# Strassen branch products: weight sums by accumulating DMAs in place of GpSimd, and the first operands split during attention

## The chip, the cores and the metric

One core of one Trainium2 chip. The metric is the device time of one execution in microseconds, as the median of several runs. TensorE (PE) multiplies matrices, VectorE (DVE), ScalarE (ACT) and GpSimd (POOL) work element by element, SyncE (SP) issues most of the loads and stores; 16 DMA engines carry them.

## The reference

One layer of a hybrid decoder: 1024 tokens, width 1024, float32. After a norm and a common input projection a state-space mixer gives `y_ssm` (width 2048) and latent attention gives `y_mla` (8 heads of 128). What the change touches is what joins them:

```
mixed = sigmoid(g_ssm) * (y_ssm @ w_branch_ssm) + sigmoid(g_mla) * (y_mla @ w_branch_mla)
h = h + mixed @ w_out
```

Norm, a two-layer MLP and a final norm follow. `w_branch_ssm` is 2048x1024 and `w_branch_mla` 1024x1024.

## The kernel before, in words

All matrix products run in float32 accuracy from pieces: every operand is split into a high part (a rounded copy, ACT, L69) and a low part (source less high part, VectorE, L70; together `split_sbuf`), and one float32 matmul is three matmuls, high by high, high by low, low by high (`mm`, L100). The stages follow one another: input projection, state-space mixer, gates, attention, branch products, out product, MLP.

**Attention** (L617 to L791) runs over 8 heads and in each over 4 pairs of 128-query tiles: scores (`sc`, `sx`), softmax on VectorE and ACT (`pr`), transposes of the probabilities on TensorE (`pp`, L737), their split (`pT`, by ACT L112 and VectorE L113), products with the values (`po`), a copy `oT` (ACT, L748), and a store to `d_o` in HBM, issued by GpSimd (L749). The state-space result lies in HBM as `d_y`, the gates as `d_g`.

**Branch products** (L798 to L943). Three products of 1024 rows of weights by 1024 tokens: `strassen(w, src, sink)` for the upper half of `w_branch_ssm` (`w_bs`) with the first half of y, the lower half with the second, and `w_branch_mla` (`w_bm`) with `d_o`. Each is cut into 2 x 2 blocks and done by seven products of 512 x 512 x 512 instead of eight, a Winograd form: F, E, G, E, G, E, E, where F, E, G are groups of four PSUM banks into which products accumulate (`pz`). A product is 48 matmuls of 128x512, 1008 in all. Its weights come as two units of 128x1024 (`st`, loaded by SP in `raw_unit` L822), its columns as two tiles `yr` (loaded in `columns` L854). Some products need sums of blocks: of the columns these are made on VectorE, of the weights on GpSimd, both in `combined` (L839): a22 + a21, then differences with a11, a12, a21, eight GpSimd instructions of 128x1024 in each `strassen`, 24 in all. `split_unit` and the `x` tiles then hold the parts; `whl` has four buffers, the units of two products; the raw weights lie in `wr` (7 buffers) and `stage` (3).

After a product, `done` hands its four banks to a sink. `set_mix` (L917) and `add_mix` (L923) write or add to `mix` in SBUF (ACT L919, VectorE L925). In the third `strassen` `gated_mix` (L931) multiplies by the gates, loaded as `g`: the sum so far once (VectorE, L935), the bank into `c` (VectorE, L937), and GpSimd adds `c` to `mix` (L938).

**Out product** (`out_row`, L985): `m`, the parts of 128 tokens of `mix` (ACT L989, VectorE L990), by `w_out`, into banks `pout`.

A scheduler of the framework sets the order of the instructions on each engine from the program's order, priorities and pools; an engine, SP's and GpSimd's queues too, takes its own instructions strictly in that order. A tile waits for the last reader of the buffer that it takes over: the pool `wr` lies where attention's tiles lay, so a first load into some of its buffers waits for the stores of `oT`.

Of the kernel before, what the change touches and what calls it, by code (L numbers as in the profile page):

```python
# [29 lines left out]
QH, NOPE, ROPE, DV = 8, 128, 64, 128  # L30
# [9 lines left out]
def hybrid_block(ctx: ExitStack, tc: tile.TileContext, a: dict):  # L40
    nc = tc.nc
    pe, act, dve, pool, sp = nc.tensor, nc.scalar, nc.vector, nc.gpsimd, nc.sync
# [7 lines left out]
    stage = ctx.enter_context(tc.tile_pool(name="stage", bufs=3))  # L50
    whl = ctx.enter_context(tc.tile_pool(name="whl", bufs=4))
# [119 lines left out]
    with ExitStack() as pa:  # L171
# [426 lines left out]
    xs = conv_x(0, first_pairs)  # L598
# [8 lines left out]
    for g in range(NG):  # L607
# [4 lines left out]
        if g + 1 < NG:  # L612
            xs = conv_x(g + 1) + conv_bc(g + 1)
    ssd.close()
    up.close()

    ring_stack = ctx.enter_context(ExitStack())  # L617
    ring_q = ring_stack.enter_context(tc.tile_pool(name="ring_q", bufs=4, reuse_waits="tile"))


    with ExitStack() as at:
# [153 lines left out]
        for n in range(4 * QH):  # L775
            h, b = divmod(n, 4)
            if b == 0 and h % 2 == 0:
                vt = values(shared["wv"], h % 4)
            scores_up_to(2 * n + 3)
            steps = weighted_values(h, b, prs[2 * n : 2 * n + 2], vt, h % 2)  # L780
            for _ in range(b + 2 >> 1):
                next(steps)
            scores_up_to(2 * n + 4)
            for _ in steps:
                pass
            if b == 1 and h + 1 < QH:
                heads_in[h + 1] = project(h + 1)
            if b == 1 and h + 2 == QH:
                at0.close()
                xr = ring_stack.enter_context(tc.tile_pool(name="xr", bufs=2, reuse_waits="tile"))  # L790
                yr = ring_stack.enter_context(tc.tile_pool(name="yr", bufs=8, reuse_waits="tile"))  # L791

# [1 line left out]


    ps2 = ctx.enter_context(ExitStack())  # L798
    pz = ps2.enter_context(tc.tile_pool(name="pz", bufs=8, space=PSUM, reuse_waits="tile"))
    with tc.using_default_side("right"):  # L800
        sm_stack = ctx.enter_context(ExitStack())
        sm = sm_stack.enter_context(tc.tile_pool(name="sm", bufs=1, reuse_waits="tile"))
# [1 line left out]
        wr = br.enter_context(tc.tile_pool(name="wr", bufs=7, reuse_waits="tile"))  # L804
# [3 lines left out]

    mix = [sm.tile([P, 8, 512], F32, name=f"mix{t}") for t in range(2)]

    def bank():
        return pz.tile([P, 512], F32, tag="z", name="pz")

    def split_unit(src):
        w = whl.tile([P, 2, 1024], F32R, tag="w", name="w")
        split_sbuf(w[:, 0, :], w[:, 1, :], src)
        return w

    def raw_unit(pl, src, k, tag):

        st = pl.tile([P, 1024], F32, tag=tag, name="st")
        sp.dma_start(out=st.rearrange("p (k c) -> p k c", k=k), in_=src.rearrange("(k p) c -> p k c", p=P))  # L822
        return st

    nx, nw = [0], [0]

    def raw_weights():
        nw[0] += 1
        return (wr, "wr") if nw[0] % 10 >= 3 else (stage, "st")

    def x_tile():
        nx[0] += 1
        if nx[0] % 6 in (1, 2):
            return xr.tile([P, 2048], F32R, tag="x", name="x")
        return ring_q.tile([P, 2112], F32R, tag="ring", name="x")[:, :2048]

    def combined(eng, op, outs, xs, ys):
        for o, x, y in zip(outs, xs, ys):
            eng.tensor_tensor(out=o, in0=x, in1=y, op=op)  # L839

    def strassen(w, src, sink):
        def weights(r, c):
            outs = []
            for q in range(2):
                pl, tag = raw_weights()
                outs.append(raw_unit(pl, w[512 * r : 512 * (r + 1), 512 * q + 256 * c : 512 * q + 256 * (c + 1)], 4, tag))
            return outs

        def columns(r, c):
            outs = []  # L850
            for kk in range(2):
                st = yr.tile([P, 1024], F32, tag="y", name="yr")
                k0 = 4 * r + 2 * kk
                sp.dma_start(  # L854
                    out=st.rearrange("p (k c) -> p k c", k=2), in_=src[:, k0 : k0 + 2, 512 * (1 - c) : 512 * (2 - c)]
                )
                outs.append(st)
            return outs

        def product(out, ws, xs, start):  # L860
            xv = []
            for x in xs:
                t = x_tile()
                split_sbuf(t[:, :1024], t[:, 1024:], x)
                xv.append(t.rearrange("p (j k c) -> p j k c", j=2, k=2))
            for g in range(2):
                wv = split_unit(ws[g]).rearrange("p j (k c) -> p j k c", k=4)
                for q in range(2):
                    o, cs = out[2 * g + q], slice(P * q, P * (q + 1))
                    for k in range(4):  # L870
                        wh, wl = wv[:, 0, k, cs], wv[:, 1, k, cs]
                        xh, xl = (xv[k // 2][:, j, k % 2, :] for j in (0, 1))
                        mm(o, wh, xh, start and k == 0, False, True)
                        mm(o, wh, xl, False, False, True)
                        mm(o, wl, xh, False, k == 3, True)

        def done(out, f, half, first):
            for g in range(2):
                for q in range(2):
                    sink(out[2 * g + q], 4 * g + 2 * f + q, 1 - half, first)  # L880

        sub, add = ALU.subtract, ALU.add
        a12, b21 = weights(1, 0), columns(1, 0)
        F = [bank() for _ in range(4)]
        product(F, a12, b21, True)
# [7 lines left out]
        for _ in range(2):  # L893
            pl, tag = raw_weights()
            s1.append(pl.tile([P, 1024], F32, tag=tag, name="s1"))
# [61 lines left out]
    ps2 = ctx.enter_context(ExitStack())  # L957
# [99 lines left out]
    with ExitStack() as us:  # L1057
# [7 lines left out]
        for g in range(DFF // 512):  # L1065
            def block(r, c, pl, tag):
                return raw_unit(pl, a["w_up"][512 * r : 512 * (r + 1), 512 * g + 256 * c : 512 * g + 256 * (c + 1)], 4, tag)

            a11, a21 = block(0, 0, su, "su"), block(0, 1, su, "su")
            a22, a12 = block(1, 1, stage, "st"), block(1, 0, su, "su")  # L1070
            E, G, F = ([bank() for _ in range(2)] for _ in range(3))

            def product(out, w, x, start):
                wv = w.rearrange("p j (k c) -> p j k c", k=4)
                for q, o in enumerate(out):
                    cs = slice(P * q, P * (q + 1))
# [62 lines left out]
            for q in range(2):  # L1139
                s = out_tile("hs")  # L1140
# [180 lines left out]
```

## Time and profile before

| | |
|---|---|
| median of 3 runs | 2233.11 us (2230.86 to 2233.98) |
| profiled execution | 2232.11 us, of it the span of the trace 2230.3 us |
| mean granted TensorE clock | 0.987 |
| TensorE, VectorE, ACT, GpSimd busy | 97%, 66%, 47%, 16% of the span |
| matmuls | 12150, of these 1008 of the branch products, 232.1 us |

The timeline counts from the start of the span. A group of instructions is named by line, engine, operation, and its tiles out<-in. "Idle before" is the time in which its engine stood still just ahead of it, with the instruction that ended the wait. The granted clock is a share of TensorE's full 2.4 GHz; 0.50 is its lower level, 1.2 GHz. For a DMA the time to landing runs from its issue until its data have arrived.

### The profile page before, as it was taken

To read this page: it belongs to the slowest core of one execution; us is meant where nothing else is said; L and a number is where in the kernel's file an instruction comes from. 1 tells how busy PE (TensorE), PEld (TensorE's weight loads), DVE (VectorE), ACT (ScalarE), POOL (GpSimd) and SP (SyncE) were. 2 spreads that over 40 slices of the span, in tenths; PEclk is the share of its full clock that TensorE was granted. 3 is DMA by queue.
4 is the path that set the end of the run, shared out by engine and by line. 5 is a ranking of instruction groups with operands and counts; after the bars stand their busy time and mean duration, and the time that the engine had idled before them with its cause. 6 is when DMAs were issued, how large, how long until landed. Compare 5 with 4: busy or idle time off the path is not lost. (4 is left out here: it accounts for less than half of the span.)

```text
span 2230.3 us, 31193 instructions
## 1 busy us (share of the span) xinstructions
PE 2160.8 (97%) x12150; PEld 1912.9 (86%) x12150; DVE 1474.1 (66%) x2094; ACT 1052.5 (47%) x1860; POOL 363.0 (16%) x400
## 2 busy tenths in 40 slices
PE   7999999999999999999998999979899999899997
PEld 7999998999989988899998888768688888688886
DVE  6542368769768677356557799954765654878776
ACT  5422255636636545367566443322454545433333
POOL 2100001202102112000000443631012221000000
PEclk9999999999999999999999999989999999999998
DMA  6444454414324334611102623461334443864442
GB/s 191 108 95 95 98 140 130 133 53 147 109 76 138 87 108 148 223 44 46 31 25 102 213 70 108 143 216 43 108 135 159 153 150 138 307 188 133 150 123 85
DMA packets 181123, 275.75 MB, mean 124 GB/s; under 512 B 18144, under 2 KB 118368, under 8 KB 180464
## 3 DMA queue, kind: packets, MB, share of 16 engines
q1 hardware_dynamic: 143376, 204.19, 28.9%
q0 software_dynamic: 37456, 69.32, 10.0%
q8 instruction: 95, 1.56, 0.3%
q14 instruction: 52, 0.43, 0.1%
q10 hardware_dynamic: 144, 0.26, 0.0%
HBM read 194.90 MB, written 78.82 MB: 123 GB/s over the span
## 5 line engine op out<-in xcount | busy, mean ns | idle before, releaser
L70 DVE TENSOR_TENSOR w<-st,w 128x1024 fp32r<-128x1024 f32 x174 | 229.6, 1320 | 183.4 <-ACT w L69 182.7
L100 PE MATMUL pm<-w,h 128*128 128x512 f32 x1344 | 307.2, 391 | 10.2 <-ACT h L69 10.2
L100 PEld LDWEIGHTS pm<-w,h 128*128 128x128 f32 x1344 | 253.6, 189 | 63.9 <-ACT h L69 11.1
L100 PE MATMUL px<-uT,w 128*128 128x346 f32 (+1 forms) x1728 | 289.8, 323 | 0.0
L100 PEld LDWEIGHTS px<-uT,w 128*128 128x128 f32 x1728 | 275.4, 188 | 1.4
L69 ACT CAST w<-st 128x1024 fp32r<-128x1024 f32 x174 | 182.4, 1049 | 137.8 <-PE pz L100 56.7
L100 PE MATMUL pz<-x,w 128*128 128x512 f32 x1008 | 232.1, 392 | 6.5 <-DVE c L937 4.1
L100 PEld LDWEIGHTS pz<-x,w 128*128 128x128 f32 x1008 | 189.5, 189 | 48.7 <-DVE w L70 5.0
L100 PE MATMUL pg<-w,uT 128*128 128x256 f32 x1536 | 195.6, 283 | 0.0
L100 PE MATMUL pg<-uT,w 128*128 128x512 f32 x768 | 195.5, 400 | 0.0
L100 PEld LDWEIGHTS pg<-w,uT 128*128 128x128 f32 x1536 | 187.7, 188 | 2.1 <-issue 0.4
L100 PE MATMUL pm<-xT,w 128*128 128x512 f32 x768 | 178.1, 389 | 0.0
L100 PEld LDWEIGHTS pm<-xT,w 128*128 128x128 f32 x768 | 144.1, 188 | 29.9
L100 PEld LDWEIGHTS pg<-uT,w 128*128 128x128 f32 x768 | 140.8, 188 | 29.9
L100 PE MATMUL pm<-xB,w 128*128 128x512 f32 x576 | 137.7, 395 | 1.6 <-DVE xT L113 1.6
L69 ACT CAST h<-hr 128x1024 fp32r<-128x1024 f32 x56 | 58.5, 1054 | 167.6 <-PE pm L100 167.6
L100 PEld LDWEIGHTS pm<-xB,w 128*128 128x128 f32 x576 | 110.1, 191 | 25.1 <-ACT w L69 1.9
L421 DVE SCALAR_TENSOR_TENSOR xs<-raw,cw,xs 128x1040 f32<-128x1040 f32 x72 | 93.1, 1298 | 12.8 <-ACT xs L419 11.8
L100 PE MATMUL pout<-w,m 128*128 128x512 f32 x384 | 92.5, 402 | 8.6 <-ACT m L989 6.9
L100 PEld LDWEIGHTS pout<-w,m 128*128 128x128 f32 x384 | 73.4, 193 | 26.1 <-ACT m L989 7.3
L513 ACT ACTIVATE m<-m,nacs 128x128 f32<-128x128 f32 x256 | 78.8, 390 | 33.3 <-DMA m<-d_acs 32.1
L561 POOL TENSOR_TENSOR prev<-prev,cdec 128x512 f32<-128x512 f32 x28 | 37.2, 1329 | 344.7 <-DVE prev L564 198.8
(269 smaller groups left out, 3692.8 us busy)
## 6 DMA issues: line engine op xcount, KB each, us to landing
st<-in_w_in SPq DMA_DIRECT2D x60, 512.0 KB, 4.3
hr<-d_h SPq DMA_DIRECT2D x56, 512.0 KB, 3.6
m<-d_acs SPq DMA_DIRECT2D x32, 512.0 KB, 3.7
st<-in_w_up SPq DMA_DIRECT2D x32, 512.0 KB, 3.8
d_h<-hs POOLq DMA_DIRECT2D x64, 256.0 KB, 3.0
st<-in_w_down SPq DMA_DIRECT2D x32, 512.0 KB, 5.2
d_h<-c POOLq DMA_DIRECT2D x48, 256.0 KB, 2.3
g<-d_g SPq DMA_DIRECT2D x44, 256.0 KB, 3.1
```

Source lines behind the costliest of these rows:

```text
L69: act.copy(out=hi, in_=src)
L70: dve.tensor_tensor(out=lo, in0=src, in1=f(hi), op=ALU.subtract)
L100: pe.matmul(out=out, lhsT=l, rhs=r, start=start, stop=stop, skip_group_check=more)
L421: dve.scalar_tensor_tensor(out=xs, in0=raw[:, k : k + L], scalar=cw[:, ct, k : k + 1], in1=xs, op0=ALU.mult, op1=ALU.add)
L513: act.activation(out=m[:, h, :], in_=m[:, h, :], func=AF.Relu, bias=nacs[:, i, hh])
L561: pool.tensor_tensor(out=heads(nxt), in0=heads(prev), in1=over(cdec, i, P), op=ALU.mult)
```

## The change

1. The sums of weights. The unit of a21 is loaded as `s`; GpSimd issues a second load onto it that adds a22 (`plus`, L878 of the new file, `accum_op=add`, 512 KB each); ACT negates the sum (`negated`, L882). `s` is then used for the third product, gets a11 added by another accumulating load for the fourth, and a12 for the fifth. A second copy of a21, `s3`, is negated and gets a11 for the sixth. So there are 8 accumulating loads in each `strassen` (24), 4 negations (12), 10 plain loads of units rather than 8 (30 for 24), and no GpSimd sum. The column sums stay on VectorE with signs changed, two of them as one fused operation each.
2. The first product's operands (`first_y`, `first_x`, `first_w`) are named and split inside the attention's last two heads; `strassen` takes them as `ready`.
3. The eight banks of `pz` become two pools of four, `pzg` for F and G, `pze` for E.

```diff
+    def block(w, r, c, q):
+        rows = w[512 * r : 512 * (r + 1), 512 * q + 256 * c : 512 * q + 256 * (c + 1)]
+        return rows.rearrange("(k p) c -> p k c", p=P)
...
+                first_y = columns(d_y[:, :8], 1, 0)
+                first_x = split_columns(first_y)
+            if b == 1 and h + 1 == QH:
+                first_w = [split_unit(w) for w in weights(a["w_bs"][:1024], 1, 0)]
...
-    pz = ps2.enter_context(tc.tile_pool(name="pz", bufs=8, space=PSUM, reuse_waits="tile"))
+    pzg = ps2.enter_context(tc.tile_pool(name="pzg", bufs=4, space=PSUM, reuse_waits="tile"))
+    pze = ps2.enter_context(tc.tile_pool(name="pze", bufs=4, space=PSUM, reuse_waits="tile"))
...
-    def combined(eng, op, outs, xs, ys):
-        for o, x, y in zip(outs, xs, ys):
-            eng.tensor_tensor(out=o, in0=x, in1=y, op=op)
...
+    def strassen(w, src, sink, ready=None):
+        def plus(outs, r, c):
+
+            for q, o in enumerate(outs):
+                pool.dma_start(out=o.rearrange("p (k c) -> p k c", k=4), in_=block(w, r, c, q), accum_op=ALU.add)
+
+        def negated(outs):
+            for o in outs:
+                act.activation(out=o, in_=o, func=AF.Copy, scale=-1.0)
...
-        a11, b11 = weights(0, 0), columns(0, 0)
-        E = [bank() for _ in range(4)]
+        s = weights(w, 0, 1)
+        plus(s, 1, 1)
+        negated(s)
+        a11, b11 = weights(w, 0, 0), columns(src, 0, 0)
+        E = banks(pze)
         product(E, a11, b11, True)
         done(E, 0, 0, False)
-        a21, a22, b12 = weights(0, 1), weights(1, 1), columns(0, 1)
-        s1 = []
...
-        combined(pool, add, s1, a21, a22)
-        combined(dve, sub, b11, b12, b11)
-        G = [bank() for _ in range(4)]
-        product(G, s1, b11, True)
+        b12 = columns(src, 0, 1)
+        minus(b11, b11, b12)
+        G = banks(pzg)
+        product(G, s, b11, True)
         done(G, 1, 1, True)
-        combined(pool, sub, a21, a11, a21)
-        combined(pool, sub, a11, s1, a11)
-        b22 = columns(1, 1)
-        combined(dve, sub, b11, b22, b11)
-        combined(dve, sub, b12, b22, b12)
-        product(E, a11, b11, False)
+        plus(s, 0, 0)
+        s3 = weights(w, 0, 1)
+        negated(s3)
+        plus(s3, 0, 0)
+        b22 = columns(src, 1, 1)
+        minus(b12, b22, b12)
+        for o, x in zip(b11, b22):
+            dve.scalar_tensor_tensor(out=o, in0=o, scalar=-1.0, in1=x, op0=ALU.mult, op1=ALU.subtract)
+        product(E, s, b11, False)
         done(E, 0, 1, True)
-        combined(pool, sub, a12, a12, a11)
-        product(G, a12, b22, False)
+        plus(s, 1, 0)
+        product(G, s, b22, False)
         done(G, 0, 1, False)
-        product(E, a21, b12, False)
+        product(E, s3, b12, False)
         done(E, 1, 1, False)
-        combined(dve, sub, b21, b21, b11)
+        a22 = weights(w, 1, 1)
+        for o, x in zip(b21, b11):
+            dve.tensor_tensor(out=o, in0=o, in1=x, op=ALU.add)
         product(E, a22, b21, False)
         done(E, 1, 0, True)
...
-    strassen(a["w_bs"][:1024], d_y[:, :8], set_mix)
+    strassen(a["w_bs"][:1024], d_y[:, :8], set_mix, (first_w, first_x, first_y))
```

The order of the instructions changes at three places. TensorE, the end of the attention; before, all branch matmuls stood behind the last `po`:

```order
L100 MATMUL po<-pTm_9246,vt 128x256 x3
L737 MATMUL pp<-ident,pr 128x128 x4
L100 MATMUL po<-pT,vt 128x256 x6
L737 MATMUL pp<-ident,pr 128x128 x3
L100 MATMUL po<-pT,vt 128x256 x13
...
L100 MATMUL po<-pT,vt 128x128
L100 MATMUL pz<-x,w 128x512 x1008
```

Now the 48 of the first product stand between `pp` and `po`, in ten pieces from right behind the last `sx` to just ahead of the last twelve `po`, and 960 behind them. The first of the pieces:

```order
L100 MATMUL sx<-kn,qn 128x344 x3
L100 MATMUL sx<-kr,qpe 128x344 x2
L100 MATMUL pz<-x,w 128x512 x6
L792 MATMUL pp<-ident,pr 128x128 x4
L100 MATMUL pz<-x,w 128x512 x3
L792 MATMUL pp<-ident,pr 128x128 x3
L100 MATMUL pz<-x,w 128x512
L100 MATMUL po<-pTm_9245,vt 128x256 x3
L100 MATMUL po<-pT,vt 128x256 x6
L792 MATMUL pp<-ident,pr 16x128
L100 MATMUL pz<-x,w 128x512 x14
```

SP's queue at the same place; before (12795 and 12797 are the second product's units a11, 12871 to 12877 those of a21 and a22):

```order
L822 DMA st_12795<-in_w_bs 128x4x256
L822 DMA st_12797<-in_w_bs 128x4x256
L822 DMA st_12871<-in_w_bs 128x4x256
L822 DMA st_12873<-in_w_bs 128x4x256
L822 DMA st_12875<-in_w_bs 128x4x256
L822 DMA st_12877<-in_w_bs 128x4x256
```

Now (12798 and 12800 are `s`, 12806 and 12808 a11, 12958 and 12960 `s3`, 13168 one of a22):

```order
L649 DMA st_12798<-in_w_bs 128x4x256
L649 DMA st_12800<-in_w_bs 128x4x256
L649 DMA st_12806<-in_w_bs 128x4x256
L649 DMA st_12808<-in_w_bs 128x4x256
L649 DMA st_12958<-in_w_bs 128x4x256
L649 DMA st_12960<-in_w_bs 128x4x256
L649 DMA st_13168<-in_w_bs 128x4x256
```

Both units of a11 moved behind both units of `s`. The load that waits for all stores of `oT`, the last one too, is the second in either list: 12797 before, 12800 now.

GpSimd's queue, from the last stores of the attention on; now, where 24 sums stood (L839):

```order
L804 DMA d_o<-oT 128x256 x9
L878 DMA st<-in_w_bs 128x4x256 x12
L878 DMA st<-in_w_bm 128x4x256 x2
L878 DMA st<-in_w_bs 128x4x256 x4
L878 DMA st<-in_w_bm 128x4x256 x2
L968 TENSOR_TENSOR mix_12741<-mix_12741,c 128x512 x2
L878 DMA st<-in_w_bm 128x4x256
```

The accumulating loads follow the last store directly; the first additions of `c` stand among those of the third `strassen`.

## Rows read from the trace of the kernel before

**Rows 1.** Page, part 1: busy us (share of the span) xinstructions.

```profile
PE 2160.8 (97%) x12150; PEld 1912.9 (86%) x12150; DVE 1474.1 (66%) x2094; ACT 1052.5 (47%) x1860; POOL 363.0 (16%) x400
```

**Rows 2.** Groups of instructions, 1228 to 1480: busy us, mean ns | idle before, releasers.

```profile
L100 PE MATMUL pz<-x,w 128*128 128x512 f32 x1008 | 232.1, 392 | 6.5 <-DVE c L937 4.1 <-DVE w L70 2.3
...
L70 DVE TENSOR_TENSOR w<-st,w 128x1024 fp32r<-128x1024 f32 x40 | 65.9, 1649 | 9.5 <-ACT w L69 9.3
...
L938 POOL TENSOR_TENSOR mix<-mix,c 128x512 f32<-128x512 f32 x28 | 50.9, 1836 | 27.1 <-DVE c L937 27.1
...
L839 POOL TENSOR_TENSOR st<-st 128x1024 f32<-128x1024 f32 x12 | 39.6, 3306 | 0.6
```

**Rows 3.** The same view of VectorE, 1500 to 1880.

```profile
L70 DVE TENSOR_TENSOR w<-st,w 128x1024 fp32r<-128x1024 f32 x32 | 39.2, 1225 | 69.9 <-ACT w L69 69.6
```

**Rows 4.** Timeline of TensorE, 1212 to 1256: start us, us, what [idle before <-releaser].

```profile
1220.24 0.91 PE L100 MATMUL po<-pT,vt 128*128 128x256 f32 x6 [1.97 <-DVE pT L113]
...
1228.84 27.45 PE L100 MATMUL pz<-x,w 128*128 128x512 f32 x120
```

**Rows 5.** Busy time by window; columns in the first line.

```profile
core 0: us, PE busy (x) PEld busy (x) DVE busy (x) ACT busy (x) POOL busy (x), PEclk, DMA share, GB/s
1215.12:1228.84 13.72, 10.65 (x75) 9.73 (x72) 11.40 (x16) 7.91 (x13) 1.08 (x2) 0.88 0.17 58
1228.84:1239.80 10.96, 10.96 (x50) 9.06 (x50) 2.52 (x3) 5.08 (x7) 0.54 (x1) 1.00 0.51 171
1235.00:1240.00 5.00, 5.00 (x23) 4.14 (x23) 1.50 (x2) 2.74 (x4) 0.00 (x0) 1.00 1.05 351
1475.00:1480.00 5.00, 3.26 (x8) 2.17 (x7) 5.00 (x5) 2.19 (x3) 1.14 (x1) 0.50 0.95 329
```

**Rows 6.** Timeline of TensorE, 1415 to 1490.

```profile
1422.18 11.17 PE L100 MATMUL pz<-x,w 128*128 128x512 f32 x48 [1.48 <-DVE w L70]
1433.61 5.73 PE L100 MATMUL pz<-x,w 128*128 128x512 f32 x24 [0.26 <-DVE w L70]
1439.88 10.95 PE L100 MATMUL pz<-x,w 128*128 128x512 f32 x46 [0.54 <-DVE w L70]
1454.96 12.49 PE L100 MATMUL pz<-x,w 128*128 128x512 f32 x48 [4.14 <-DVE c L937]
1474.32 1.22 PE L100 MATMUL pout<-w,m 128*128 128x512 f32 x2 [6.87 <-ACT m L989]
1477.28 12.91 PE L100 MATMUL pout<-w,m 128*128 128x512 f32 x46 [1.74 <-DVE m L990]
```

**Rows 7.** Timeline of ACT, 1228 to 1240.

```profile
1229.04 0.37 ACT L748 COPY oT<-po 128x256 f32<-128x256 f32 x1 [1.58 <-PE po L100]
...
1237.07 1.05 ACT L69 CAST w<-st 128x1024 fp32r<-128x1024 f32 x1 [1.92 <-DMA st<-in_w_bs]
```

**Rows 8.** Waits of SP's queue, 1215 to 1260: us in total, times, longest.

```profile
SPq L822 <- DMA d_o<-oT: 10.4, 1, 10.4
```

**Rows 9.** Timeline of SP's queue, 1225 to 1236.

```profile
1233.45 2.73 SPq L822 DMA_DIRECT2D st<-in_w_bs  x5
```

**Rows 10.** DMA issues, 1225 to 1240: xcount, KB each, median us to landing.

```profile
st<-in_w_bs SPq DMA_DIRECT2D x5, 512.0 KB, 6.5
```

**Rows 11.** Groups of instructions of VectorE, 1361 to 1398.

```profile
L839 DVE TENSOR_TENSOR yr<-yr 128x1024 f32<-128x1024 f32 x6 | 12.9, 2163 | 0.0
L70 DVE TENSOR_TENSOR x<-yr,x 128x1024 fp32r<-128x1024 f32 x5 | 11.4, 2276 | 0.6 <-ACT x L69 0.6
L70 DVE TENSOR_TENSOR w<-st,w 128x1024 fp32r<-128x1024 f32 x5 | 8.7, 1738 | 0.0
```

**Rows 12.** Timeline of ACT, 1460 to 1478.

```profile
1473.21 2.00 ACT L989 ACTIVATE m<-mix 128x1024 fp32r<-128x1024 f32 x2 [4.68 <-DVE c L937]
```

**Rows 13.** DMA issues of the whole span, from GpSimd's queue.

```profile
cq<-d_cq POOLq DMA_DIRECT2D x1, 4096.0 KB, 14.9
qpe<-d_qp POOLq DMA_DIRECT2D x8, 512.0 KB, 4.0
```

More of the change, by code (lines that the diff above doesn't have):

```diff
@@ L615, in hybrid_block, with split_unit, raw_unit, raw_weights @@
     up.close()
+    def split_unit(src):
+        w = whl.tile([P, 2, 1024], F32R, tag="w", name="w")
+        split_sbuf(w[:, 0, :], w[:, 1, :], src)
+        return w
+    def raw_unit(pl, src, k, tag):
+        st = pl.tile([P, 1024], F32, tag=tag, name="st")
+        sp.dma_start(out=st.rearrange("p (k c) -> p k c", k=k), in_=src.rearrange("(k p) c -> p k c", p=P))
+        return st
+    nx, nw = [0], [0]
+    def raw_weights():
+        nw[0] += 1
+        return (wr, "wr") if nw[0] % 10 >= 3 else (stage, "st")
+    def x_tile():
+        nx[0] += 1
+        if nx[0] % 6 in (1, 2):
+            return xr.tile([P, 2048], F32R, tag="x", name="x")
+        return ring_q.tile([P, 2112], F32R, tag="ring", name="x")[:, :2048]
+    def block(w, r, c, q):
+        rows = w[512 * r : 512 * (r + 1), 512 * q + 256 * c : 512 * q + 256 * (c + 1)]
+        return rows.rearrange("(k p) c -> p k c", p=P)
+    def weights(w, r, c):
+        outs = []
+        for q in range(2):
+            pl, tag = raw_weights()
+            st = pl.tile([P, 1024], F32, tag=tag, name="st")
+            sp.dma_start(out=st.rearrange("p (k c) -> p k c", k=4), in_=block(w, r, c, q))
+            outs.append(st)
+        return outs
+    def columns(src, r, c):
+        outs = []
+        for kk in range(2):
+            st = yr.tile([P, 1024], F32, tag="y", name="yr")
+            k0 = 4 * r + 2 * kk
+            sp.dma_start(
+                out=st.rearrange("p (k c) -> p k c", k=2), in_=src[:, k0 : k0 + 2, 512 * (1 - c) : 512 * (2 - c)]
+            )
+            outs.append(st)
+        return outs
+    def split_columns(xs):
+        outs = []
+        for x in xs:
+            t = x_tile()
+            split_sbuf(t[:, :1024], t[:, 1024:], x)
+            outs.append(t.rearrange("p (j k c) -> p j k c", j=2, k=2))
+        return outs
     ring_stack = ctx.enter_context(ExitStack())
@@ L809, in hybrid_block @@
     mix = [sm.tile([P, 8, 512], F32, name=f"mix{t}") for t in range(2)]
[L811 to L835, printed above, removed]
-    def combined(eng, op, outs, xs, ys):
-        for o, x, y in zip(outs, xs, ys):
-            eng.tensor_tensor(out=o, in0=x, in1=y, op=op)
[L841 to L865, printed above, removed]
@@ new lines, in banks, with product @@
+    def banks(pl):
+        return [pl.tile([P, 512], F32, tag="z", name="pz") for _ in range(4)]
+    def strassen(w, src, sink, ready=None):
[5 more added lines that the diff above has]
+                act.activation(out=o, in_=o, func=AF.Copy, scale=-1.0)
+        def product(out, ws, xs, start, ready=None):
+            xv = ready[1] if ready else split_columns(xs)
@@ L866, in product @@
             for g in range(2):
-                wv = split_unit(ws[g]).rearrange("p j (k c) -> p j k c", k=4)
+                wv = (ready[0][g] if ready else split_unit(ws[g])).rearrange("p j (k c) -> p j k c", k=4)
                 for q in range(2):
@@ L880, in done, with minus @@
                     sink(out[2 * g + q], 4 * g + 2 * f + q, 1 - half, first)
[L882 to L885, printed above, removed]
-        done(F, 0, 0, True)
-        a11, b11 = weights(0, 0), columns(0, 0)
-        E = [bank() for _ in range(4)]
+        def minus(outs, xs, ys):
+            for o, x, y in zip(outs, xs, ys):
+                dve.tensor_tensor(out=o, in0=x, in1=y, op=ALU.subtract)
@@ L889, in strassen @@
+        if ready:
+            a12, b21 = None, ready[2]
+        else:
+            a12, b21 = weights(w, 1, 0), columns(src, 1, 0)
+        F = banks(pzg)
+        product(F, a12, b21, True, ready)
+        done(F, 0, 0, True)
+        s = weights(w, 0, 1)
[3 more added lines that the diff above has]
+        E = banks(pze)
         product(E, a11, b11, True)
         done(E, 0, 0, False)
-        a21, a22, b12 = weights(0, 1), weights(1, 1), columns(0, 1)
@@ L892, in strassen @@
-        s1 = []
-        for _ in range(2):
-            pl, tag = raw_weights()
-            s1.append(pl.tile([P, 1024], F32, tag=tag, name="s1"))
-        combined(pool, add, s1, a21, a22)
-        combined(dve, sub, b11, b12, b11)
-        G = [bank() for _ in range(4)]
-        product(G, s1, b11, True)
-        done(G, 1, 1, True)
-        combined(pool, sub, a21, a11, a21)
-        combined(pool, sub, a11, s1, a11)
-        b22 = columns(1, 1)
-        combined(dve, sub, b11, b22, b11)
-        combined(dve, sub, b12, b22, b12)
```

## The prediction

> **What bounds the kernel now.** I read the page's engine table first. TensorE is busy 97% of the span and GpSimd 16% [rows 1], so the 24 sums that leave GpSimd are worth nothing by themselves; they count only where GpSimd makes another engine late and that engine makes TensorE wait. So I went to the stretch that the change touches, from the end of the attention to the first matmuls of the out product, and read its groups [rows 2]: 1008 branch matmuls, 6.5 us of TensorE idle among them, all of it put down to VectorE (c at L937, the low parts at L70). The reader should see that VectorE's w splits take 1649 ns there and 1225 ns in the later MLP stretch, for the same shape [rows 2, 3]: they are stretched, and the GpSimd groups in the same table (L839 3.3 us each, L938 1.8 us each) are what runs beside them.
>
> TensorE's timeline says where the idle time lies. From 1228.84 on the branch matmuls run without a gap, 120 in the first 27.45 us [rows 4], 10.96 us for the 48 of a product at full clock [rows 5]; every loss is at the far end, in the third product: idle 1.48, 0.26, 0.54 and 4.14 us, and after the last product 6.87 and 1.74 us before the out product [rows 6]. So two places decide: the end of the attention, where the order of TensorE changes, and the end of the third product, where relief of VectorE could be cashed.
>
> **Part 1: the first product moves into the attention.** Its 48 matmuls (10.96 us) now stand among the last transposes and `po` matmuls. From 1215.12 to 1228.84 TensorE is busy 10.65 of 13.72 us at a mean granted clock of 0.88 [rows 5]: 3.1 us of idle time (the longest 1.97 us, for DVE pT [rows 4]) and about 10.65 x 0.12 = 1.3 us of lost clock are there to be filled. That the work fits into these holes is my choice, since ten pieces of it are spread over them; the other bound is that nothing is filled, because the transposes queue behind matmuls and the softmax chain gets later by as much. So the attention ends 11.0 - 4.4 = 6.6 us later (up to 11.0 us), at about 1235.4 instead of 1228.8.
>
> **Part 2: the second product has lost its cover.** Before, the attention's last result was copied at 1229.04 [rows 7], written out, and a weights load that waits for all these writes (the queue sat 10.4 us on it [rows 8]) went out at 1233.45, first of five that take 2.73 us to issue [rows 9]. It landed by 1237.07, when ACT could cast it [rows 7], 3.6 us after its issue. All this passed under the first product, which lasted until 1239.80 [rows 5]. The waiting load was the *second* unit of the second product's weights; the first had gone out early. Now the waiting load is the second unit of s, and *both* units of a11, the second product's weights, stand behind it on SP's queue, with the first product already spent. Counting from the end of the `po` matmuls: 4.45 us to the first load (1233.45 less about 1229.0), 0.55 us to the next (2.73 / 5), its landing, a cast of 1.05 us [rows 7] and a low part of 1.22 us [rows 3], of which the first two matmuls of the product need nothing (0.3 us off). For the landing the first of the burst took 3.6 us and the median of the five is 6.5 us [rows 10]; a11's first unit is second in its burst, so I take 4.9 us. That is 11.9 us: the second product begins at 1247.3 instead of 1239.8, **7.5 us late**.
>
> After such a hole the clock is down. After the holes of 6.87 and 1.74 us the granted clock was 0.50, its lower level, in 1475 to 1480 [rows 5], and 46 matmuls took 12.91 us [rows 6] where 46 x 0.2284 = 10.5 would do: 2.4 us. After 4.14 us idle 48 took 12.49 us [rows 6], 1.5 us more. I take 2.4 us. The start costs **+9.9 us**; bounds +7.7 (landing 3.6, clock 1.5) and +15.9 (landing 6.5, nothing filled in the attention).
>
> The accumulating load of s's first unit is issued by GpSimd right after the last d_o write, before and beside this burst. In 1235 to 1240 the DMA engines moved 351 GB/s at a share of 1.05 [rows 5], so they were full. By the Trainium skill (DMA: Bandwidth & Descriptors, Issuing engines are not separate DMA queues) transfers of all issuers share the same 16 engines and interleave, which speaks against moving sums to DMAs here: half a megabyte more at 351 GB/s would put an estimated 1.5 us on a11's landing, and the sum below would be 1.5 us higher. No row has an accumulating transfer, so the landing of 4.9 us stays.
>
> **Part 3: GpSimd's sums go.** 24 L839 instructions, 12 of them at 3306 ns [rows 2], leave. In 1361 to 1398 eight of them run in the third product, and VectorE's groups there average 2163 (6 instructions), 2276 (5) and 1738 ns (5) [rows 11] against 1225 ns [rows 3]: 5.6 + 5.3 + 2.6 = **13.5 us** of VectorE time that comes back. VectorE's count of operations does not change (the b sums stay, two of them in another form), and the L938 additions stay. At 1422 VectorE is 1.5 us late and at 1454.96 4.1 us late [rows 6], less than 13.5. So I let the idle time of 6.4 us and the 1.5 us of clock behind the longest piece go: **-7.9 us** (bounds: nothing, if the L938 additions alone keep VectorE full; no more than 7.9). In the first two products TensorE never waits, so the relief there is worth nothing; if their cover were gone, the 16 other sums would matter.
>
> **Part 4: into the out product.** Its first operand m waited for c (L937) and was ready 6.87 us after the last branch matmul, its low part 1.74 us later [rows 6, 12]. With VectorE in time there remain one c (0.7), m's two parts (1.05 and 1.2 to 1.75) and the hand-overs, 3.6 to 5.5 us of the 8.6. I take **-3.5 us** (bounds -2 and -8.6). The half clock after it stays.
>
> **Part 5: what comes new, at nothing.** 24 accumulating DMAs, 24 less GpSimd sums, six more loads and 12 negations on ACT (12 x 1.05 = 12.6 us). ACT's are hidden: under the first product it was busy 5.08 of 10.96 us [rows 5]. An accumulating DMA is in no row. Below, it is a plain load of the same size from GpSimd's queue: 4.0 us; above, the 4 MB load of that queue: 14.9 us [rows 13]. It has about 22 us (two products) between the split that reads the old sum and the product that needs the new one, as there are weight buffers for two products; less issue, negation, cast and low part some 17 us. Nearest is the row of equal size, so 5 to 7 us and no stall. As a stream, eight in a Strassen product of 7 x 10.96 = 76.7 us may take 9.6 us each.
>
> **Sum.** 2232.1 (the profiled execution's own time) + 9.9 - 7.9 - 3.5 = 2230.6 us. The median of the runs shown is 1.0 us above that execution, so the forecast is **2231.6 us**, against 2233.1: no change that a measurement of this kernel can tell (0.2%, 4.5 us).
>
> **Rivals.**
> *The wait into the out product vanishes altogether (faster).* With VectorE 13.5 us ahead, m could be ready under the last product: -8.6 in place of -3.5, and no hole for the clock to fall in (-2.4). Against it: m waited for c, the reader of the last banks. 2231.6 - 7.5 = 2224 us. A start at its low bound (+7.7) with the full -7.9 and -5.5 gives 2228 and also counts here.
> *VectorE stays late (slower).* In 1361 to 1398 it ran without a pause, but in the third product's second half it works beside the L938 additions, 28 x 1836 ns [rows 2], not beside L839. If those alone set its pace, both gains are zero and only the start is left: 2233.1 + 9.9 = 2243 us. It decides if VectorE, at 1422, is still over 1.5 us behind TensorE's need. For it: over the whole stretch the w splits average 1649 ns, and L839 fills a third of it at most (24 x 3.3 of 250 us). Against it: 13.5 us is three times the lateness.
> *Accumulating DMAs are slow (slower).* One at a time and over 9.6 us each they pace the products: at 12 us, 3 x (96 - 76.7) = 58 us, so 2291 us. For it: each reads and writes its target; against it: 4.0 us for the plain one.
> *The change does little.* The first operands were split during the attention before, too; if the scheduler's order gives the first product no holes to fill but a11 lands under the attention's late end, start and end are both near zero: 2233 us.
>
> **How the numbers follow.** Forecast 0.52, by its bounds 2227 to 2238 us (0.12 of it below 2228.6, 0.02 above 2237.6); the hole vanishing or the cheap start 0.20, faster; VectorE late 0.15 (0.13 slower, 0.02 same for a cheaper start); slow DMAs 0.08; little change 0.05. So faster 0.32, same 0.45, slower 0.23. The range 2222 to 2243 us leaves out the slow DMAs, the dearest start without gains and the lowest corner, under 0.2.
>
> **What would show it.** Right: `po` ends 6 to 7 us later than before; then one hole of 10 to 13 us on TensorE that ends with ACT's cast or VectorE's low part of a11, and a granted clock at 0.5 behind it; VectorE's x and w splits near 1.2 us in the third product before the L938 additions begin; no pz idle over 1 us near its end; under 6 us to the out product; accumulating DMAs landing in 4 to 8 us. Wrong: a hole under 5 us at the start, a pz wait on an accumulating DMA or ACT's negation, or VectorE still the releaser of the 4 us hole.

## The result, and the profile after

| | before | changed |
|---|---|---|
| median | 2233.11 us (2230.86 to 2233.98) | 2245.58 us (2241.31 to 2248.38), 5 runs |
| profiled execution, span | 2232.11, 2230.3 us | 2245.58, 2243.8 us |
| mean granted clock | 0.987 | 0.984 |

The ratio is 1.0056, interval 1.0041 to 1.0071: slower by 12.5 us. The forecast was 2231.6, its range ended at 2243. Of the twelve executions of `plain` below one took 10861.59 us: it is in the median of 2231.45 us given there (the other eleven have 2230.70 us) but not in the ratio.

TensorE's timeline of the changed kernel, from the end of the attention to the out product, where [rows 4] and [rows 6] stood (start, length, what, idle before and its releaser):

```profile
1233.22 1.48 PE L100 MATMUL po<-pT,vt 128*128 128x256 f32 x12
1245.86 23.99 PE L100 MATMUL pz<-x,w 128*128 128x512 f32 x96 [11.16 <-ACT w L69]
1274.08 9.53 PE L100 MATMUL pz<-x,w 128*128 128x512 f32 x26 [4.23 <-ACT w L69]
1284.14 11.21 PE L100 MATMUL pz<-x,w 128*128 128x512 f32 x48 [0.53 <-DVE w L70]
1295.77 4.40 PE L100 MATMUL pz<-x,w 128*128 128x512 f32 x18 [0.43 <-DVE w L70]
...
1312.35 152.63 PE L100 MATMUL pz<-x,w 128*128 128x512 f32 x672 [0.40 <-DVE mix L955]
1467.50 12.78 PE L100 MATMUL pz<-x,w 128*128 128x512 f32 x48 [2.52 <-DVE c L967]
1488.46 1.22 PE L100 MATMUL pout<-w,m 128*128 128x512 f32 x2 [8.19 <-ACT m L1019]
1491.42 18.88 PE L100 MATMUL pout<-w,m 128*128 128x512 f32 x72 [1.74 <-DVE m L1020]
```

The account, at 0.2284 us for a matmul at full clock (10.96 us for 48, [rows 5]): the second product begins at 1245.86 instead of 1239.80, +6.1, and its 96 matmuls take 23.99 instead of 21.9, +2.1. Then come losses that stood nowhere before: 4.23 us ahead of the fourth product, 26 matmuls in 9.53 us instead of 5.9 behind it (+3.6; the granted clock of 1275 to 1280, below, was 0.50, the lower of its two levels, 1.2 GHz), 0.53 and 0.43: +8.8. The end of the third strassen loses 0.40 + 2.52 + 1.8 (12.78 less 10.96) = 4.7 where it lost 7.9 [rows 6]: -3.2. The way into the out product is 9.9 us for 8.6: +1.3. The sum is 15.0; the traces are 14.1 us apart at the second piece of the out product (1491.42 less 1477.28), the spans 13.5. So 0.9 us of the sum is not accounted for. The window, with the columns of [rows 5]:

```profile
1275.00:1280.00 5.00, 4.96 (x12) 3.70 (x12) 0.29 (x1) 1.89 (x2) 1.28 (x1) 0.50 1.24 198
```

What TensorE waits for at 1274 is a cast on ACT, and ACT waits for a load. ACT's timeline, and behind it GpSimd's (L878 are the accumulating loads):

```profile
1272.98 1.04 ACT L69 CAST w<-st 128x1024 fp32r<-128x1024 f32 x1 [10.21 <-DMA st<-in_w_bs]
```

```profile
1256.48 1.29 POOL L878 DMA_DIRECT2D st<-in_w_bs  x1 [2.60 <-DVE w L70]
1267.06 1.28 POOL L878 DMA_DIRECT2D st<-in_w_bs  x1 [9.29 <-issue]
1270.56 2.59 POOL L878 DMA_DIRECT2D st<-in_w_bs  x2 [2.21 <-DMA st<-in_w_bs]
```

Over all 24, the line L878 has these times to landing:

```profile
DMA to landing us min/median/max: 5.7/7.8/16.4
```

The load issued at 1256.48 adds a11 to the first unit of s for the fourth product. It went out as soon as the low part that reads the old sum was made, and from there TensorE had 13.4 us of work left: it ran dry at 1269.85 (1245.86 + 23.99). Then GpSimd issues two loads of the next strassen, and at 1271.8 that of the second unit. The view of DMA issues from 1255 to 1258 has that one load with its time to landing, 16.4 us, and the view from 1234 to 1300 has the ten that GpSimd issues there, median 10.5 us:

```profile
st<-in_w_bs POOLq DMA_DIRECT2D x1, 512.0 KB, 16.4
```

```profile
st<-in_w_bs SPq DMA_DIRECT2D x12, 512.0 KB, 7.5
st<-in_w_bs POOLq DMA_DIRECT2D x10, 512.0 KB, 10.5
```

The third strassen did get its VectorE time back. The groups of VectorE in 1374 to 1411, the stretch that answers to [rows 11]:

```profile
L70 DVE TENSOR_TENSOR w<-st,w 128x1024 fp32r<-128x1024 f32 x7 | 8.5, 1217 | 4.5 <-ACT w L69 4.5
L70 DVE TENSOR_TENSOR x<-yr,x 128x1024 fp32r<-128x1024 f32 x7 | 8.5, 1216 | 4.0 <-ACT x L69 4.0
```

1217 and 1216 ns where the groups took 1738 and 2276, and VectorE now idles there. At the very end it waits for gates. VectorE's timeline:

```profile
1471.81 0.69 DVE L965 SCALAR_TENSOR_TENSOR mix<-g,mix 128x512 f32<-128x512 f32 x1 [3.86 <-DMA g<-d_g]
...
1480.13 0.69 DVE L965 SCALAR_TENSOR_TENSOR mix<-g,mix 128x512 f32<-128x512 f32 x1 [2.24 <-DMA g<-d_g]
1480.74 1.28 DVE L967 SCALAR_TENSOR_TENSOR c<-g,pz 128x512 f32<-128x512 f32 x2
...
1484.30 0.69 DVE L965 SCALAR_TENSOR_TENSOR mix<-g,mix 128x512 f32<-128x512 f32 x1 [2.28 <-DMA g<-d_g]
...
1486.04 1.28 DVE L967 SCALAR_TENSOR_TENSOR c<-g,pz 128x512 f32<-128x512 f32 x2
```

A gate load needs one of four buffers, which c (L967) and the operation of L965 free; the last c ends 7.0 us after the last branch matmul (1467.50 + 12.78 = 1480.28).

### The profile page after: what moved, and what is told of

Read it like the earlier page. It is cut to its first block, busy times and chain, and to the rows that moved or that the text cites. A ratio compares the mean times of both kernels' runs of the same rounds, so it can differ in the third digit from the quotient of the medians.

```text
span 2243.8 us, 31246 instructions
## 1 busy us (share of the span) xinstructions
PE 2163.5 (96%) x12150; PEld 1914.9 (85%) x12150; DVE 1434.3 (64%) x2094; ACT 1062.3 (47%) x1872; POOL 314.7 (14%) x400
## 3 DMA queue, kind: packets, MB, share of 16 engines
q0 software_dynamic: 50128, 81.90, 13.5%
## 4 chain that ended last, share of the span: by engine, by line
PE 85%; issue 5%; DMA 5%; DVE 4%; ACT 1%; POOL 0%; SPq 0%; DVEq 0%; POOLq 0%; ACTq 0%
PE pm L100 26%; PE pg L100 16%; PE px L100 12%; PE pz L100 5%; PE pout L100 4%; PE pq L100 4%; PE po L100 3%; PE sc L100 3%; PE pd L571 2%; DMA st<-in_w_bs 2%; PE pb L100 1%; PE pp L792 1%; DMA g<-d_g 1%; PE ps L100 1%; PE pr L100 1%
## 5 line engine op out<-in xcount | busy, mean ns | idle before, releaser
L100 PEld LDWEIGHTS pm<-w,h 128*128 128x128 f32 x1344 | 253.5, 189 | 64.0 <-ACT h L69 11.2
L69 ACT CAST w<-st 128x1024 fp32r<-128x1024 f32 x180 | 188.6, 1049 | 156.8 <-DMA st<-in_w_bs 39.7
L100 PE MATMUL pz<-x,w 128*128 128x512 f32 x1008 | 239.3, 398 | 19.3 <-ACT w L69 15.4
L70 DVE TENSOR_TENSOR h<-hr,h 128x1024 fp32r<-128x1024 f32 x56 | 68.1, 1221 | 36.9 <-ACT h L69 36.9
```

Of the source, the lines that this page charges most:

```text
L100: pe.matmul(out=out, lhsT=l, rhs=r, start=start, stop=stop, skip_group_check=more)
```

## The experiments

After the result the theory was: splitting the PSUM pool, not the early splitting of operands, moves the first product; the accumulating loads hold the DMA engines too long; the end is the gates'. Each median below is compared with runs of the kernel before on the same chip, 2231.0 to 2231.9 us.

### What moves the first product

```diff
-    pz = ps2.enter_context(tc.tile_pool(name="pz", bufs=8, space=PSUM, reuse_waits="tile"))
+    pzg = ps2.enter_context(tc.tile_pool(name="pzg", bufs=4, space=PSUM, reuse_waits="tile"))
+    pze = ps2.enter_context(tc.tile_pool(name="pze", bufs=4, space=PSUM, reuse_waits="tile"))
```

> The kernel before with one line changed: the eight banks of pz become pools of four, pzg for F and G, pze for E. Sums stay on GpSimd, no operand is named early. Theory (the split of the pools, and not the early splitting of operands, moves the first product into the attention): po ends 5 to 6 us later than before, all 48 matmuls of the first product inside; the second product then waits on TensorE for its weights, but its first unit is the load that does not wait for the last store, so the hole is 3 to 8 us, less than the 11.2 of the changed kernel; no stall at the fourth product; 2236 to 2241 us. Rival (the split of the pools is nothing, the early operands are the cause): as before, 2231 to 2235 us.

2237.84 us, ratio 1.0025 (1.0014 to 1.0035). The first product stands inside the attention in the same pieces as with the change, and the second pays:

```profile
1241.29 24.33 PE L100 MATMUL pz<-x,w 128*128 128x512 f32 x98 [8.04 <-ACT w L69]
```

The theory held; its hole of 8.0 us is at the upper end, and the third strassen loses as before (4.12 us to c, 6.80 + 1.74 to the out product). The counterpart leaves out the change's second part and keeps the rest:

```diff
-                first_y = columns(d_y[:, :8], 1, 0)
-                first_x = split_columns(first_y)
-            if b == 1 and h + 1 == QH:
-                first_w = [split_unit(w) for w in weights(a["w_bs"][:1024], 1, 0)]
...
-    strassen(a["w_bs"][:1024], d_y[:, :8], set_mix, (first_w, first_x, first_y))
+    strassen(a["w_bs"][:1024], d_y[:, :8], set_mix)
```

> The changed kernel without its second part: the first product's operands are no longer named and split inside the attention; accumulating loads and the two pools stay. Theory (that part does nothing, the operands were split there before and the split pools alone move the first product): the first product stays inside the attention, hole of 10.5 to 11.5 us, 2242 to 2248 us, as the changed kernel. Rival (the early operands cost the start): hole under 8 us, 2240 us or less.

2247.00 us, 1.0074 (1.0058 to 1.0089), hole 10.90 us. The early operands do nothing; the pools move the product.

### What the accumulating loads cost

One line of `plus`:

```diff
-                pool.dma_start(out=o.rearrange("p (k c) -> p k c", k=4), in_=block(w, r, c, q), accum_op=ALU.add)
+                pool.dma_start(out=o.rearrange("p (k c) -> p k c", k=4), in_=block(w, r, c, q))
```

> The changed kernel with the 24 accumulating loads as plain loads of the same blocks from GpSimd's queue: it leaves out the additions, so the weight sums are single blocks. Theory (an accumulating load holds the DMA engines about twice as long as a plain one, 195 GB/s against 370 to 390, and from 1240 to 1280 they are full): landing from 7.8 us median to 4 to 5.5, the stall of 4.2 us at the fourth product and its 3.6 us of lost clock gone, the hole of 11.2 us unchanged; 2236 to 2240 us. Rival (the chain load, accumulate, negate, split through GpSimd and ACT is too long whatever the transfer does): the stall stays within 1 us, 2243 to 2248 us.

2231.45 us, 0.9998 (0.9989 to 1.0008): lower than was expected. One flag in one line separates this from 2245.58, and the whole net loss goes with it. TensorE, from the attention's end on:

```profile
1245.85 219.77 PE L100 MATMUL pz<-x,w 128*128 128x512 f32 x960 [10.98 <-ACT w L69]
1472.85 1.22 PE L100 MATMUL pout<-w,m 128*128 128x512 f32 x2 [7.22 <-ACT m L1019]
1475.81 24.48 PE L100 MATMUL pout<-w,m 128*128 128x512 f32 x93 [1.75 <-DVE m L1020]
```

The hole at the start is unchanged, and behind it 960 matmuls run without a wait, the third strassen included. That leaves two readings: the transfer itself is long, or it fills the engines. So each accumulating load became two plain ones:

```diff
-                pool.dma_start(out=o.rearrange("p (k c) -> p k c", k=4), in_=block(w, r, c, q), accum_op=ALU.add)
+                pool.dma_start(out=o.rearrange("p (k c) -> p k c", k=4), in_=block(w, r, c, q))
+                t = again.tile([P, 1024], F32, tag="again", name="again")
+                pool.dma_start(out=t.rearrange("p (k c) -> p k c", k=4), in_=block(w, r, c, q))
```

> The changed kernel with each accumulating load replaced by two plain loads of the same block, one into its tile and one into a spare tile that nobody reads (two spare tiles); it leaves out the additions. A plain load moves 350 GB/s where the accumulating ones moved 195 alone and 240 to 260 in the mixture, so two plain ones hold the engines about as long as one accumulating. Theory (it is the time on the DMA engines that makes the weights late): the stalls at the third to fifth product come back, ACT w 3 us or more behind the hole of 11 us; 2238 to 2247 us. Rival (it is the longer way of the one accumulating transfer, not the engines' load): no pz wait but the 11 us, as with plain loads, 2229 to 2235 us.

2245.64 us, 1.0060 (1.0047 to 1.0073), the time of the changed kernel. Its waits:

```profile
1249.88 24.19 PE L100 MATMUL pz<-x,w 128*128 128x512 f32 x96 [14.02 <-ACT w L69]
1274.79 1.20 PE L100 MATMUL pz<-x,w 128*128 128x512 f32 x4 [0.73 <-ACT w L69]
...
1283.00 6.08 PE L100 MATMUL pz<-x,w 128*128 128x512 f32 x24 [1.89 <-ACT w L69]
1291.65 181.42 PE L100 MATMUL pz<-x,w 128*128 128x512 f32 x792 [2.56 <-ACT w L69]
```

Nobody reads the second load, yet stalls for weights are back. That they come by the DMA engines is seen on the other queue: the plain loads that SP issues in 1234 to 1300 land later in `plain_twice` (the second line) than in `plain` (the first), though the spare loads are not on it:

```profile
st<-in_w_bs SPq DMA_DIRECT2D x15, 512.0 KB, 5.5
```

```profile
st<-in_w_bs SPq DMA_DIRECT2D x13, 512.0 KB, 12.2
```

They are not the same stalls as in the changed kernel, however: the spare loads also go out earlier than the accumulating ones did, and lengthen the hole by 3 us. And they stand in GpSimd's own queue, which waited 15.1 us in 1235 to 1300 for their two tiles. So the run does not separate the engines from that queue in size, and it is partly chance that the two times agree to 0.1 us. The busy time by window of 1240 to 1280, of the changed kernel, of `plain` and of `plain_twice`; the last two columns are the DMA engines' share and GB/s:

```profile
1240.00:1280.00 40.00, 29.87 (x109) 23.54 (x110) 11.06 (x11) 14.24 (x15) 11.64 (x9) 0.80 1.16 265
```

```profile
1240.00:1280.00 40.00, 34.15 (x142) 28.10 (x143) 15.78 (x15) 20.79 (x24) 7.53 (x10) 0.88 0.92 309
```

```profile
1240.00:1280.00 40.00, 29.14 (x116) 23.25 (x117) 13.42 (x13) 17.48 (x20) 10.46 (x14) 0.83 1.04 351
```

Full engines move 351 GB/s of plain loads and 265 of the mixture here. Whether the cost hangs on the place was asked with accumulating loads in the last two strassens alone:

```diff
-in_=block(w, r, c, q), accum_op=ALU.add)
+in_=block(w, r, c, q), **({} if ready else dict(accum_op=ALU.add)))
```

> The changed kernel with plain loads in place of the eight accumulating ones of the first strassen alone; the other sixteen accumulate. It leaves out the additions of the first strassen. Theory (the accumulating loads cost TensorE time only where the DMA engines are full, in the 40 us after the attention): as with all 24 plain, the stall at the fourth product gone, landing of the sixteen 5.5 to 7.5 us, no pz wait on them; 2230 to 2235 us. Rival (each accumulating load costs, wherever it stands): two thirds of the 14 us remain, 2239 us or more.

2237.55 us, 1.0025 (1.0015 to 1.0035): between the two. By the ratios the first strassen's eight cost about 7 us (1.0056 less 1.0025) and the other sixteen about 6 (1.0025 less 0.9998), each known to some 3 us, and what TensorE still waits for is 0.50 + 0.52 us at the fourth product, 2.02 us for weights ahead of the fourteenth, and 2.13 us for c ahead of the last half product. The theory fell in its "only": eight in the crowd after the attention cost about as much as sixteen behind it, and those are not free.

### The two parts apart

```diff
-    pzg = ps2.enter_context(tc.tile_pool(name="pzg", bufs=4, space=PSUM, reuse_waits="tile"))
-    pze = ps2.enter_context(tc.tile_pool(name="pze", bufs=4, space=PSUM, reuse_waits="tile"))
+    pzg = pze = ps2.enter_context(tc.tile_pool(name="pz", bufs=8, space=PSUM, reuse_waits="tile"))
```

> The changed kernel with one pool of eight banks again; accumulating loads and early operands stay. Theory: the first product stands behind the attention again and covers most of the second product's load; the hole at its start is 1 to 3 us in place of 11.2, with less lost clock, and the fourth product's stall shrinks or goes, since the accumulating loads start at the same time after the attention but TensorE needs them 5 us later; 2233 to 2239 us. Rival (the loss is the accumulating loads'): 2241 us or more, with the stall at the fourth product as large as before (4 us and the clock behind it).

This is the change without its third part. 2242.91 us, 1.0054 (1.0042 to 1.0066): the rival's side. The first product is behind the attention again, the hole is 0.77 us, and the stalls have moved:

```profile
1240.66 22.43 PE L100 MATMUL pz<-x,w 128*128 128x512 f32 x96 [0.77 <-ACT w L69]
1265.20 7.68 PE L100 MATMUL pz<-x,w 128*128 128x512 f32 x24 [2.12 <-ACT w L69]
1281.72 106.21 PE L100 MATMUL pz<-x,w 128*128 128x512 f32 x456 [8.83 <-ACT w L69]
```

TensorE reaches the fourth product earlier and waits there longer for the same loads, 2.12 us for the first unit and 8.83 for the second. With this edit and the plain loads of above together:

> The changed kernel with one pool of eight banks and all 24 accumulating loads as plain ones: it leaves out the additions. Theory (split pools cost the start some 8 to 10 us, accumulating loads 14 us, and the third strassen gains 6 to 8 us whatever carries the sums, the wait before the out product being the gates'): hole at the start under 2 us, no pz wait over 1 us, 6 to 8.5 + 1.7 us before the out product; 2221 to 2226 us. Rival (with the first product behind the attention the loads pile up later and cost the same): 2230 us or more.

2224.25 us, 0.9968 (0.9955 to 0.9980): hole 0.49 us, no other pz wait, 8.43 + 1.74 us to the out product. Between this and `plain` lie about 7 us (0.9968 against 0.9998), the price of the uncovered start where nothing else delays the loads.

### What the sums on GpSimd cost at all

The kernel before without its GpSimd sums; `s1` is the tile of a21:

```diff
-        combined(pool, add, s1, a21, a22)
...
-        combined(pool, sub, a21, a11, a21)
-        combined(pool, sub, a11, s1, a11)
...
-        combined(pool, sub, a12, a12, a11)
```

> The kernel before with the 24 GpSimd sums left out, products taken on the single blocks; all else as before. Theory: this is all that the sums cost, the 6.4 us of pz idle time and its 1.5 us of clock in the third strassen, the 8.6 us before the out product staying: 2223 to 2227 us. Rival (VectorE stays late by the additions of c on GpSimd): pz idle of 4 us or more stays, 2228 us or more.

2221.73 us, 0.9950 (0.9937 to 0.9964), 10 us less than before, somewhat more than expected, since the wait before the out product shrank as well, from 6.87 to 5.22 us:

```profile
1230.86 228.72 PE L100 MATMUL pz<-x,w 128*128 128x512 f32 x1008
1464.80 1.22 PE L100 MATMUL pout<-w,m 128*128 128x512 f32 x2 [5.22 <-ACT m L984]
```

All 1008 matmuls without a wait. This is what a way to make the sums free could bring here.

### The end

```diff
-        gp = br.enter_context(tc.tile_pool(name="gp", bufs=4, reuse_waits="tile"))
+        gp = br.enter_context(tc.tile_pool(name="gp", bufs=8, reuse_waits="tile"))
```

> The changed kernel with eight buffers gp for the gates in place of four. Theory (the wait before the out product is the chain of gate loads, each of which waits for a buffer that c frees): VectorE no longer waits for g at the end (18.5 us before), the idle time before the out product falls from 8.2 + 1.7 to 3 to 5 us, the last pz wait of 2.5 us goes; 2238 to 2242 us. Rival (VectorE and GpSimd's additions are late by themselves): the 8.2 us stay within 1 us, 2243 to 2248 us.

2246.00 us, 1.0062 (1.0050 to 1.0074). The mechanism is right and the gain is not: the wait before the out product fell from 8.19 to 2.09 us, but c ahead of the last product went from 2.52 to 4.72, and behind the attention a second stall of 4.55 us came up. The same edit on the kernel before:

> The kernel before with eight gate buffers gp instead of four, nothing else. Theory (the wait before the out product is the chain of gate loads): 6.87 + 1.74 us fall to 3.5 to 5, the pz waits stay; 2226 to 2230 us. Rival (four more gate loads in the burst after the attention make weights late, as they seem to have with the change): a pz wait on ACT w near 1240 to 1265 that eats the gain, 2231 to 2236 us.

2231.27 us, 0.9999 (0.9991 to 1.0008):

```profile
1460.92 13.25 PE L100 MATMUL pz<-x,w 128*128 128x512 f32 x48 [8.16 <-DVE c L937]
1476.27 0.72 PE L100 MATMUL pout<-w,m 128*128 128x512 f32 x2 [2.10 <-ACT m L989]
1478.57 21.66 PE L100 MATMUL pout<-w,m 128*128 128x512 f32 x86 [1.58 <-DVE m L990]
```

Behind the attention nothing is late here; the wait has only changed its place, from the out product to the last product, which needs the banks that c reads. VectorE's timeline shows why:

```profile
1456.01 0.69 DVE L935 SCALAR_TENSOR_TENSOR mix<-g,mix 128x512 f32<-128x512 f32 x1 [2.17 <-DMA g<-d_g]
...
1459.49 0.69 DVE L935 SCALAR_TENSOR_TENSOR mix<-g,mix 128x512 f32<-128x512 f32 x1 [1.05 <-DMA g<-d_g]
1460.10 0.68 DVE L937 SCALAR_TENSOR_TENSOR c<-g,pz 128x512 f32<-128x512 f32 x1
```

With more buffers the scheduler puts the L935 of the last banks ahead of the c that TensorE needs, and they wait for their gates.

### Accumulating loads where VectorE is short, and there alone

The kernel before, with GpSimd's sums in the first two strassens and the accumulating form in the third:

```diff
-    def strassen(w, src, sink):
+    def strassen(w, src, sink, loaded=False):
...
+        if not loaded:
...
+        else:
+            s = weights(0, 1)
+            plus(s, 1, 1)
+            negated(s)
...
-    strassen(a["w_bm"], d_o, gated_mix)
+    strassen(a["w_bm"], d_o, gated_mix, True)
```

Under `not loaded` stands the body of before, under `else` that of the change.

> The kernel before with the sums of the third strassen alone by accumulating loads; one pool, order and GpSimd sums of the first two as before. Theory (the gain that was forecast lies in the third strassen, where GpSimd's sums stretch VectorE's splits, and there the DMA engines have room): the pz idle time of 6.4 us falls under 1.5, the start is as before, the wait before the out product stays at 8 to 9 us; 2223 to 2227 us. Rival (the accumulating loads make the weights of the third strassen late as they did in the first): pz waits for ACT w of 3 us or more there, 2230 us or more.

2230.26 us, 0.9995 (0.9987 to 1.0004). The w waits at 1422 to 1440 are gone, but a wait of 2.72 us for ACT w has come at 1375, c is still 3.60 us late at 1456, and the out product waits 8.39 + 1.74 us: partly the rival's case. With this and the eight gate buffers:

> The two edits together, third strassen by accumulating loads and eight gate buffers. Theory: the gains add, 2217 to 2223 us. Rival (with VectorE in time the buffers gain nothing, or the burst eats it): as the third strassen alone, 2223 us or more.

2223.84 us, 0.9971 (0.9963 to 0.9980), faster than before by 7 us and than the changed kernel by 22. From the profiled run, the slowest of its eleven:

```profile
1456.72 13.66 PE L100 MATMUL pz<-x,w 128*128 128x512 f32 x48 [5.70 <-DVE c L986]
1472.47 1.22 PE L100 MATMUL pout<-w,m 128*128 128x512 f32 x2 [2.10 <-ACT m L1038]
1474.78 25.52 PE L100 MATMUL pout<-w,m 128*128 128x512 f32 x101 [1.09 <-DVE m L1039]
```

The gains of the two edits are zero each alone and 0.3% together. I have no run that shows why they need each other.

## Why the prediction was wrong

*Part 1, right.* `po` ended 5.7 us later (1234.7 for 1229.0), forecast 6.6. The reason given by the change's words was not the cause, though: the pools were (`pools_only`, `no_early`). The order of the instructions had shown the move, so the sum did not suffer.

*Part 2, right in mechanism, high in size.* Hole 11.2 us (forecast 11.9), second product 6.1 us late (7.5), lost clock 2.1 us (2.4): 8.2 for 9.9. The units of a11 stood behind those of s, as read.

*Part 3, right where the loads leave it alone.* -7.9 was forecast; with plain loads, or without sums, no pz matmul of the third strassen waits at all. In the changed kernel -3.2 us were left, c being 2.5 us late.

*Part 4, wrong.* Forecast -3.5, measured +1.3. The step "with VectorE in time there remain one c, m's two parts and the hand-overs" looked at VectorE and not at the gates: even with no pz wait in the third strassen the out product waited 7.22 + 1.75 us (`plain`), and 5.22 + 1.73 with no sums at all (`before_nosums`). The trace of before showed VectorE idle for g there, in rows that I did not use:

```profile
1465.91 0.69 DVE L935 SCALAR_TENSOR_TENSOR mix<-g,mix 128x512 f32<-128x512 f32 x1 [2.16 <-DMA g<-d_g]
...
1470.15 0.69 DVE L935 SCALAR_TENSOR_TENSOR mix<-g,mix 128x512 f32<-128x512 f32 x1 [2.36 <-DMA g<-d_g]
```

*Part 5, the step that failed.* "Nearest is the row of equal size, so 5 to 7 us and no stall." The 5 to 7 us fit only the quickest accumulating loads (5.7 us at the least, median of all 24 7.8), and I took the time to landing for the whole cost, not the time on the DMA engines. Ten of them in 42 us, beside the loads of two strassens, wanted about twice a plain load's share of engines that [rows 5] had shown to be full in 1235 to 1240. They landed in 10.5 us, the one that mattered first in 16.4. The 17 us that I allowed it were wrong too: they count from a split two products ahead, but the sum for the third product itself came late, its split was made one product ahead, and from the issue to TensorE's running dry there were 13.4 us. So the term that was put at nothing measured 8.8 us at the fourth and fifth products, and leaving out the flag alone gave all 14 us back. This was also the sign of being wrong that the prediction names, a pz wait on an accumulating DMA. Without Part 5's error the sum comes out: `plain` ran in 2231.45 us, where 2231.6 was forecast. That it came so close is luck, since Part 2 was 1.7 us too high and Part 4 some 4 us too low (-3.5 for 8.97 less 8.61).

*The rivals.* Slow accumulating loads came true in kind, with 0.08 and a price of 58 us: too little chance, since the threshold of 9.6 us each was taken over a whole strassen, whereas the loads are issued in bursts; and too high a price, since the bursts end. VectorE staying late named about the right size (2243) for a wrong reason. The wait into the out product did not vanish, it grew; the corner that the prediction adds up to 2228 us there comes to 2227.4 (2233.1 + 7.7 - 7.9 - 5.5), which changes no chance.

## What to carry to other kernels

A DMA that adds is paid for on the DMA engines, not on the engine that it relieves: by the rates of this case count it as about two plain transfers, and look at the share of the engines in the 40 us in which it must land, not at the mean of 124 GB/s over the span. Put such loads where the relieved engine is the bound and the queues are quiet; here even that gained nothing alone (`third_acc`, 0.9995) and 0.3% only with more gate buffers. And when a work item moves ahead of its old place, look at what it used to cover.

## What the hardware showed

An accumulating load of 512 KB holds the engines about twice as long as a plain one. With one in flight and nothing else, in 1336 to 1338 of the changed kernel, the engines are fully busy (share 1.14) and move 181 GB/s; with nothing but accumulating loads in flight, in 1275 to 1280 (the row in the section on the result), 198 GB/s at a share of 1.24. Plain loads moved 351 GB/s at 1.05 [rows 5]. The first of these windows:

```profile
1336.00:1338.00 2.00, 2.00 (x10) 1.65 (x10) 0.90 (x1) 2.00 (x3) 0.00 (x0) 1.00 1.14 181
```

The Trainium skill (DMA: Bandwidth & Descriptors, Rules for kernel authors) says that an accumulate reads its destination and writes it later; the half rate agrees with a second trip over the same bytes. GpSimd also takes longer to issue one: the lines of L878 with the flag and without it, smallest, median and largest in ns:

```profile
L878 POOL DMA_DIRECT2D st<-in_w_bs x16: 1274/1283/1839, 1242.2 to 1355.5; - x16
```

```profile
L878 POOL DMA_DIRECT2D st<-in_w_bs x16: 748/751/763, 1242.4 to 1340.4; - x16
```

What stays open is how much of the loss is the order of GpSimd's queue. The second unit's load for the fourth product was issued at 1271.8, although its tile was free at 1261.6: ahead of it stood two loads of the next strassen, which waited for plain loads of SP that took up to 21.7 us to land. Its low part was made by 1284.1, so with the first unit in time TensorE would have stood at the product's second half instead (24 matmuls from 1269.85 on end at 1275.3), as it did in `one_pool`. In `plain` the same order cost nothing (issued at 1265.2, no wait). So as far as these runs show, the accumulating loads make the delay and the order passes it on; a version with that order changed was not tried.
